# An expert layer on one core: rows gathered whole and then turned, weight pieces split in one instruction per part

## The chip, the cores and the metric

The kernel runs on one core of a Trainium2 chip. The metric is device time in microseconds: the median of the timed runs of the kernel as it stands is 1961.04 us (three runs, 1960.67 to 1962.01 us). All numbers of the profile are from one profiled execution, whose span is 1961.2 us.

## The reference

Two encoder layers over 256 tokens of width 1024. Each has a token mixer, a cross-attention into 256 memory tokens and a channel mixer, every one of them followed by a layer norm of the residual. The channel mixer of the first layer is dense; that of the second sends each token to two of eight experts. The file that is given ends with the cross-attention; the change touches the experts alone, and what they compute is this:

```
logits = x @ moe_router                # 256 tokens x 8 experts
top 2 of 8, gates = softmax of the two logits
expert e: y = (silu(x @ moe_wg[e]) * (x @ moe_wu[e])) @ moe_wd[e]
x <- LayerNorm(ALPHA * x + sum over the two experts of gate * y)
```

An expert's hidden width is 3584, so its three matrices hold 3 x 1024 x 3584 float32 numbers, 42 MiB; the eight experts hold 336 MiB, and all of it is read once.

## The kernel before

Products are made at more than the precision of TensorE's fast float32 form: a factor is held as a rounded part h and the rest l, in the type float32r, and a product is the sum of three matmuls, h by h, h by l and l by h. Weights come from memory as float32 and are split on the chip.

**Weight pieces.** `wload` (L294 to L321) loads one piece of 1 MiB (128 partitions x 2048) into the next buffer `wr` of a ring, copies it on ScalarE to the rounded part `wh` (L312) and subtracts that on VectorE to get `wl` (L316). It does so in steps of n // pieces columns; in the expert stage `pieces[0]` is `PX`, which is 4, so a piece takes four ScalarE and four VectorE instructions of 128x512. The parts have a ring of four buffers of their own, `wr` in the expert stage one of eleven: two for the whole kernel, one that held keys, five of the second layer and `NX` = 3 of this stage. SyncE issues the load when VectorE has finished with the buffer.

**Experts.** `moe` (L1270 on) ranks the experts, gives each token a slot in its expert's list, and then runs eight experts of up to 128 tokens. Per expert:

- `gather` (L1333): `pd` is a 0/1 matrix that puts tokens into slots. The tokens' two parts (`xtokh`, `xtokl`) are stationary in pieces of 128x128 and `pd` is streamed, so that the result `xg` comes out turned, features on the partitions (L1344, 32 matmuls of 128 columns); four ScalarE copies bring it to SBUF (L1346).
- `gate_up` (L1355), seven times, 512 hidden columns at a time: 48 matmuls of 512 columns on two pieces of `moe_wg` and two of `moe_wu` (L1363 to L1365), then `hs` = silu(gate) * up (ScalarE L1368, VectorE L1369).
- `down` (L1372), one step later: four transposes of `hs` (L1375), a split of the result into `hh` and `hl` (L408), 24 matmuls on two pieces of `moe_wd` into `ps_ye` (L1387 to L1389). The second piece of the very last step is put behind the split of the hidden part.
- `combine` (L1391), after the seventh: `ps_ye`, scaled by the gates, is split (`yh` ScalarE, `yl` VectorE, L1409 and L1410) and spread to the tokens (`ps_co`, L1413 and L1414), and VectorE adds it to `x` (L1417, L1419) and makes the matrix `pg` of the next combine (L1395).

A scheduler sets the order of instructions on each engine when the program is built; each engine then takes its own list strictly in order and waits on semaphores. The next expert's gather is called at step `NC - 3` of seven, and its instructions stand among those of the running expert.

Of the kernel before, what the change touches and what calls it, by code (L numbers as in the profile page):

```python
# [19 lines left out]
P = 128  # L20
# [17 lines left out]
PM, PC, PX = 2, 4, 4  # L38
# [6 lines left out]
NX = 3  # L45
# [76 lines left out]
def _tiles():  # L122
    """name -> (index, first k-tile, k-tiles, first column, columns) of the pieces in which a weight is loaded"""
    def feat(i, c0, n):
        return [(i, 0, KT, c0 + c, min(256, n - c)) for c in range(0, n, 256)]

    def tok(i, c0, n):
        return [(i, k, 4, c0 + c, min(512, n - c)) for c in range(0, n, 512) for k in (0, 4)]

    def down(i, n):  # L130
        return [(i, k, 2, 0, D) for k in range(0, n // P, 2)]

    t = {"w_in": [], "ffn_wd": down(0, D_FF)}
    for l in range(L):
        for f in (0, AW, 2 * AW):
            t["w_in"] += feat(l, f, AW)
        t["w_in"] += tok(l, 3 * AW, AW) + [(l, 0, KT, 4 * AW, 24)] + feat(l, 2968, CW)
        for c, n in ((1560, 512), (2072, 384), (2456, 512), (3224, 256)):
            t["w_in"] += tok(l, c, n)
    for n in ("xq", "xk"):  # L140
        t[n] = [x for l in range(L) for x in feat(l, 0, D)]
    for n in ("xv", "xo", "w_out"):
        t[n] = [x for l in range(L) for x in tok(l, 0, D)]
    for n in ("ffn_wg", "ffn_wu"):
        t[n] = feat(0, 0, D_FF)
    for n in ("moe_wg", "moe_wu"):
        t[n] = [x for e in range(NE) for x in tok(e, 0, FE)]
    t["moe_wd"] = [x for e in range(NE) for x in down(e, FE)]
    return t
# [13 lines left out]
def tile_encoder(ctx: ExitStack, tc: tile.TileContext, a: dict, out: bass.AP, cw: dict):  # L163
# [20 lines left out]
    def abank(name):  # L184
        """the banks of psa and psf in turn"""
        turn[0] = (turn[0] + 1) % 4
        return bank(psa, "pa", name) if turn[0] else bank(psf, "pf", name)

# [9 lines left out]
    @contextmanager  # L198
    def weights(name, bufs=2, side="left", ring=parts):
        """adds buffers to the ring of weight parts, or of weights as loaded"""  # L200
        with tc.tile_pool(name="W" + name, bufs=bufs, side=side, reuse_waits="tile") as pool:
            ring += [pool] * bufs
            yield
            ring[:] = [r for r in ring if r is not pool]
# [54 lines left out]
    def load_rest(M):  # L259
        SY.dma_start(x, a["x"].rearrange("(h p) d -> p h d", p=P))  # L260
        w = (w0 + w1) // 2
        for i, nm in enumerate(("rt32", "wm")):
            t = M.tile([P, 32, 32], F32, name=nm).rearrange("p a b -> p (a b)")[:, :w]
            SY.dma_start(t, a["consts"][:, n0 + i * w:n0 + i * w + w])
            V.tensor_copy(hm_all[:, i * w:i * w + w], t)
        rt = M.tile([P, 256], F32, name="tm32")[:, :KT * NE].rearrange("p (k e) -> p k e", k=KT)
        SY.dma_start(rt, a["moe_router"][0].rearrange("(k p) e -> p k e", p=P))
        V.tensor_copy(rth, rt)
        V.tensor_sub(rtl, rt, R_(rth))
        # lower bound of the second layer  # L270
        lbt = M.tile([P, 32, 32], F32, name="rb").rearrange("p a b -> p (a b)")[:, :2 * CW].rearrange("p (i c) -> p i c", i=2)
        SY.dma_start(lbt, a["lbl"][None].to_broadcast([P, 2, CW]))
        V.tensor_max(lb[:, 0], lbt[:, 0], lbt[:, 1])
        V.tensor_sub(lbt[:, 0], lbt[:, 0], lb[:, 0])
        V.tensor_sub(lbt[:, 1], lbt[:, 1], lb[:, 0])
        A.activation(lbt, lbt, AF.Exp)
        V.tensor_add(lb[:, 0], lbt[:, 0], lbt[:, 1])
        V.reciprocal(lb[:, 1], lb[:, 0])
        V.tensor_mul(lb[:, 0], lbt[:, 1], lb[:, 1])
        V.tensor_scalar(lb[:, 1], lb[:, 0], -1.0, 1.0, op0=OP.mult, op1=OP.add)  # L280
# [9 lines left out]
    where = _offsets()  # L290

    def wload(name, i, k0, n0, c0, n1, late=()):
        """late: instructions behind which the parts are taken"""
# [8 lines left out]
        # behind a norm only the first weights may be split before it ends  # L302
# [20 lines left out]
    def wload_halves(name, i, k0, n0, c0, n1, cols):  # L323
        """a piece of weights as two halves of its columns or of its k-tiles, in small buffers"""
        n = n0 * n1
        raw = rotate(raws).tile([P, 2048], F32, name="wr")
        at = where[name, i, k0, n0, c0, n1]
        SY.dma_start(raw[:, :n], a[name][at:at + P * n].rearrange("(p n) -> p n", p=P))
        raw = raw[:, :n].rearrange("p (a b) -> p a b", a=n0)
        for j in range(2):  # L330
            W = halves[0]
            src = raw[:, :, j * n1 // 2:(j + 1) * n1 // 2] if cols else raw[:, j * n0 // 2:(j + 1) * n0 // 2]
            m = n0 if cols else n0 // 2
            h, l = (W.tile([P, 1024], F32R, name=t)[:, :n // 2].rearrange("p (a b) -> p a b", a=m) for t in ("hh", "hl"))
            A.activation(h, src, AF.Copy)
            V.tensor_sub(l[:, :m // 2], src[:, :m // 2], R_(h[:, :m // 2]))
            G.tensor_sub(l[:, m // 2:], src[:, m // 2:], R_(h[:, m // 2:]))
            yield h, l
# [5 lines left out]
    def together(*parts):  # L344
        """interleaves generators that yield the share of their work that is done"""
# [9 lines left out]
    def later(gen, n):  # L355
        """the steps of a generator as if they stood n instructions further down"""
# [13 lines left out]
    def proj_feat_steps(name, i, c0, ncol, xh, xl, evac, bank_=None):  # L370
        """out^T[f, tok]: weights stationary"""
# [38 lines left out]
    def rms_rstd(dst, ss, n, bias=None):  # L410
        """dst = (ss / n + eps) ** -0.5"""
# [15 lines left out]
    def log_sig(dst, src):  # L427
        """dst = ln(1 + exp(-src)) = -ln(sigmoid(src))"""
# [7 lines left out]
    def mixer(l, xh, xl, kctx):  # L436
        wi = ("w_in", l)
        with tc.tile_pool(name=f"mx{l}", bufs=1, reuse_waits="tile") as M, ExitStack() as mctx:
# [32 lines left out]
            def unit(f0, n):  # L471
                """l2 norm of the heads of conv tiles f0 .. f0 + n"""
# [10 lines left out]
            def products(w, f0):  # L483
                """k of a chunk against its tiles f0 .. f0 + 3, heads of either parity in a bank"""
# [11 lines left out]
            def A1():  # L496
# [28 lines left out]
                # (I + L^T)^-1 of the 32-blocks: 96 blocks side by side on the partitions  # L525
# [34 lines left out]
            def A1c(LT, wm):  # L560
# [37 lines left out]
            def A1b(beta, ld, DB):  # L598
# [38 lines left out]
            def A2(k_t, v_t, beta, ef, cdp, fb, AT, U64, col_b):  # L637
                # u', w'^T, k decays
# [37 lines left out]
                # state recurrence  # L676
# [30 lines left out]
                # outputs  # L707
# [76 lines left out]
            # C projections  # L784
# [97 lines left out]
    def softmax_rows(M, ps, n, scale, pt):  # L882
        """ps [P, n, 256] logits in PSUM -> pt [P, n, 256] probabilities"""
# [62 lines left out]
    def mixer_c(l, MS, big, c2, g2, M, sg, qc, ci, cg, oc):  # L946
# [27 lines left out]
        # chunk decays and the decayed queries  # L974
# [17 lines left out]
        # state recurrence  # L992
# [30 lines left out]
        for hf in range(NH):  # L1023
            tok = slice(hf * P, hf * P + P)
            # at a level, the left half of a block is key to the right one going forward, and the right
            # half to the left one going backward: both directions meet in one product
# [73 lines left out]
    def affine(e, x, mean, rstd, lp):  # L1100
        """x <- (x - mean) * rstd * gain + bias"""
# [8 lines left out]
    def resid_ln(l, i, pool, srcs, rows_ready=None, parts=None):  # L1110
        """x <- LN(ALPHA x + y); srcs(add, norm) calls add(hf, c, ps) for every [P, 512] piece of y and
        norm(hf) when a half is complete. Returns x^T in two parts. rows_ready(hf): x itself is
        wanted early."""
# [33 lines left out]
    def tok_out(w, xh, xl):  # L1147
        def srcs(add, norm):
            ws = [[wload(*w, kh * 4, 4, c * 512, 512) for kh in range(2)] for c in range(2)]
            pss = [[bank(psb, "pb", "ps_t") for _ in range(2)] for _ in range(NH)]  # L1150
            # the end of the second half comes behind the first half, whose norm it covers
# [118 lines left out]
    def moe(l, i, xh, xl, xth, xtl):  # L1270
        with weights("r3", NX, ring=raws), tc.tile_pool(name="mo", bufs=1, reuse_waits="tile") as O:
# [19 lines left out]
            # experts ahead of an expert: a larger logit, or the same one and a lower index  # L1291
# [41 lines left out]
            def gather(e, sl):  # L1333
# [5 lines left out]
                for i, src in enumerate((xth, xtl)):  # L1339
                    for k0 in (0, 4):  # L1340
                        pg = bank(psb, "pb", "ps_gt").rearrange("p (k t) -> p k t", k=4)
                        for k in range(4):
                            for hf in range(NH):
                                T.matmul(pg[:, k], src[:, hf, (k0 + k) * P:(k0 + k + 1) * P], pd[:, hf],  # L1344
                                         start=hf == 0, stop=hf == NH - 1)
                        A.activation(g[:, i, k0:k0 + 4], pg, AF.Copy)  # L1346
                return g[:, 0], g[:, 1]

            def expert_run(experts, sl, late=False):
                """the down projection of a step follows the gate / up projection of the next one"""  # L1350
# [21 lines left out]
                def down(e, c, hs, ye):  # L1372
# [6 lines left out]
                    for f0 in (0, 2):  # L1379
                        # behind the last loads the hidden part goes first  # L1380
# [10 lines left out]
                def combine(e, ye, first):  # L1391
                    # a token takes the row of its slot, weighted by its gate
# [54 lines left out]
            # the statistics of the last norm are taken anew where an expert has more tokens than slots  # L1447
# [103 lines left out]
```

## Time and profile before

| | |
|---|---|
| median of the runs | 1961.04 us (1960.67 to 1962.01) |
| span of the profiled execution | 1961.2 us |
| busy: TensorE, VectorE, ScalarE, GpSimd | 94%, 80%, 65%, 13% |
| expert stage | about 926 to 1943 us of the span |
| expert stage, 1000 to 1100 us: TensorE, VectorE, ScalarE | 99.55, 92.13, 80.05 us of 100 |
| memory traffic there | 349 GB/s, DMA engines 95% busy |

The page gives busy time by engine and by group of instructions. A busy TensorE is one on which matmuls overlap, so the spacing of their starts says more than their durations. The stage of the experts is read from the windows, the waits and the timeline, since the shares of the whole span mix it with the two mixers.

### The profile page before, as it was taken

What the parts mean: (1) busy time and instruction counts of PE and PEld (TensorE: products, weight loads), DVE (VectorE), ACT (ScalarE), POOL (GpSimd) and SP (SyncE); (2) the same over time, 40 slices, a digit from 0 to 9 for tenths busy, and PEclk for the clock granted to TensorE, in tenths of its full rate; (3) what the DMA queues carried; (4) which work ended last, traced back from release to release, by engine and by line L of the source; (5) the groups of instructions that cost most, each with busy time, mean ns of one, the idle gap of its engine ahead of it and who ended that gap; (6) DMA issues with size and microseconds to landing.
All of it is one profiled execution on the core that took longest, in us unless ns stands there. A gap on an engine that the chain in (4) does not pass through costs nothing. (4 is left out here: it accounts for less than half of the span.)

```text
span 1961.2 us, 31715 instructions
## 1 busy us (share of the span) xinstructions
PE 1838.9 (94%) x11906; PEld 1544.8 (79%) x11906; DVE 1575.2 (80%) x2812; ACT 1277.4 (65%) x2559; POOL 257.4 (13%) x248
## 2 busy tenths in 40 slices
PE   6889999999979898998999999999999999999996
PEld 5778779899967777686888788887888878788784
DVE  7887665755578966665889989899899898998986
ACT  4755435555536544454788778787877877787774
POOL 4545310000036353001000000000000000000000
PEclk8988999999989888998999999999999999999998
DMA  6321255555323313552999999999999989999980
GB/s 217 111 101 67 90 190 206 176 180 185 126 81 119 103 67 108 215 215 95 350 354 354 346 357 342 354 350 350 346 350 354 351 335 358 339 353 343 347 349 23
DMA packets 71266, 473.44 MB, mean 241 GB/s; under 512 B 8768, under 2 KB 12224, under 8 KB 15936
## 3 DMA queue, kind: packets, MB, share of 16 engines
q1 hardware_dynamic: 70384, 466.09, 64.6%
q10 hardware_dynamic: 720, 5.24, 0.7%
q8 instruction: 95, 1.56, 0.3%
q14 instruction: 67, 0.55, 0.1%
HBM read 470.26 MB, written 1.05 MB: 240 GB/s over the span
## 5 line engine op out<-in xcount | busy, mean ns | idle before, releaser
L316 DVE TENSOR_TENSOR wl<-wr,wh 128x512 fp32r<-128x512 f32 (+2 forms) x1622 | 1017.6, 693 | 119.3 <-ACT wh L312 116.8
L312 ACT ACTIVATE wh<-wr 128x512 fp32r<-128x512 f32 (+1 forms) x1656 | 915.0, 630 | 241.1 <-PE ps_gu L1365 152.2
L1364 PE MATMUL ps_gu<-wl,xg 128*128 128x512 f32 x896 | 352.8, 395 | 0.1
L1363 PE MATMUL ps_gu<-wh,xg 128*128 128x512 f32 x896 | 350.9, 397 | 0.0
L1365 PE MATMUL ps_gu<-wh,xg 128*128 128x512 f32 x896 | 350.6, 392 | 0.0
L1364 PEld LDWEIGHTS ps_gu<-wl,xg 128*128 128x128 f32 x896 | 169.0, 189 | 37.8 <-DVE wl L316 2.3
L1363 PEld LDWEIGHTS ps_gu<-wh,xg 128*128 128x128 f32 x896 | 169.1, 189 | 36.8 <-ACT wh L312 0.5
L1365 PEld LDWEIGHTS ps_gu<-wh,xg 128*128 128x128 f32 x896 | 168.8, 188 | 36.9
L1387 PE MATMUL ps_ye<-wh,hh 128*128 128x512 f32 x448 | 176.7, 396 | 4.6 <-ACT hh L408 4.6
L1388 PE MATMUL ps_ye<-wl,hh 128*128 128x512 f32 x448 | 176.6, 394 | 0.0
L1389 PE MATMUL ps_ye<-wh,hl 128*128 128x512 f32 x448 | 169.8, 397 | 0.0
L319 POOL TENSOR_TENSOR wl<-wr,wh 128x384 fp32r<-128x384 f32 (+6 forms) x68 | 103.6, 1544 | 290.4 <-ACT wh L312 290.1
L1475 POOL TENSOR_TENSOR x<-x,lp 128x512 f32<-128x512 f32 x1 | 1.8, 1817 | 1029.2 <-ACT x L1474 1029.2
L1387 PEld LDWEIGHTS ps_ye<-wh,hh 128*128 128x128 f32 x448 | 84.2, 188 | 26.7 <-ACT hh L408 7.9
L1257 PE MATMUL ps_gu<-xTl,wh 128*128 128x256 f32 x352 | 99.1, 282 | 0.0
L1388 PEld LDWEIGHTS ps_ye<-wl,hh 128*128 128x128 f32 x448 | 84.3, 188 | 18.6
L1256 PE MATMUL ps_gu<-xTh,wh 128*128 128x256 f32 x352 | 98.8, 282 | 0.0
L1258 PE MATMUL ps_gu<-xTh,wl 128*128 128x256 f32 x352 | 98.8, 281 | 0.0
L1389 PEld LDWEIGHTS ps_ye<-wh,hl 128*128 128x128 f32 x448 | 82.5, 188 | 17.3
L1257 PEld LDWEIGHTS ps_gu<-xTl,wh 128*128 128x128 f32 x352 | 66.7, 189 | 0.6 <-DVE xTl L408 0.2
L1256 PEld LDWEIGHTS ps_gu<-xTh,wh 128*128 128x128 f32 x352 | 66.7, 190 | 0.5
L1258 PEld LDWEIGHTS ps_gu<-xTh,wl 128*128 128x128 f32 x352 | 66.8, 190 | 0.0
(451 smaller groups left out, 3276.9 us busy)
## 6 DMA issues: line engine op xcount, KB each, us to landing
wr<-in_moe_wg_dram SPq DMA_DIRECT2D x112, 1024.0 KB, 6.8
wr<-in_moe_wu_dram SPq DMA_DIRECT2D x112, 1024.0 KB, 6.9
wr<-in_moe_wd_dram SPq DMA_DIRECT2D x112, 1024.0 KB, 7.0
wr<-in_w_in_dram SPq DMA_DIRECT2D x16, 1024.0 KB, 4.9
wr<-in_ffn_wg_dram SPq DMA_DIRECT2D x11, 1024.0 KB, 5.2
wr<-in_ffn_wu_dram SPq DMA_DIRECT2D x11, 1024.0 KB, 5.0
wr<-in_ffn_wd_dram SPq DMA_DIRECT2D x11, 1024.0 KB, 4.9
wr<-in_xk_dram SPq DMA_DIRECT2D x8, 1024.0 KB, 4.9
```

What stands on the lines that cost most here:

```text
L312: A.activation(h[:, s], raw[:, s], AF.Copy)
L316: V.tensor_sub(l[:, m], raw[:, m], R_(h[:, m]))
L319: G.tensor_sub(l[:, m], raw[:, m], R_(h[:, m]))
L1256: T.matmul(ps[:, g], wh[:, k, fs], xh[:, k, :], start=k == 0, stop=False)
L1257: T.matmul(ps[:, g], wh[:, k, fs], xl[:, k, :], start=False, stop=False)
L1258: T.matmul(ps[:, g], wl[:, k, fs], xh[:, k, :], start=False, stop=k == KT - 1)
L1363: T.matmul(pt, gh[:, k], wh[:, k4], start=k == 0, stop=False)
L1364: T.matmul(pt, gh[:, k], wl[:, k4], start=False, stop=False)
L1365: T.matmul(pt, gl[:, k], wh[:, k4], start=False, stop=k == KT - 1)
L1387: T.matmul(ye[n], hh[:, f0 + f], dh[:, f, ns], start=b, stop=False)
L1388: T.matmul(ye[n], hh[:, f0 + f], dl[:, f, ns], start=False, stop=False)
L1389: T.matmul(ye[n], hl[:, f0 + f], dh[:, f, ns], start=False, stop=z)
```

## The change

The step count of the split in the expert stage goes from `PX` = 4 to 1: a piece takes one ScalarE and one VectorE instruction of 128x2048. `NX` goes from 3 to 2, so that the ring of loads has ten buffers. The 8 KiB per partition that this frees hold, among other things, the new tile `rows`.

`gather` now keeps `pd` stationary and streams the tokens' parts, 512 features at a time, summing the h and the l part in one bank: eight matmuls of 512 columns give an expert's tokens as whole float32 rows. Two ScalarE copies bring them to `rows`, eight transposes of 128x128 turn them, and two calls of `evac_split` (ScalarE copy and VectorE subtraction, L408) make the two parts of `xg` again. Of the rest of the diff nothing reaches the program: comments and texts are gone.

```diff
-PM, PC, PX = 2, 4, 4
+PM, PC, PX = 2, 4, 1
...
-NX = 3
+NX = 2
...
                 g = act.tile([P, 2, KT, P], F32R, name="xg", tag="opTh" if e % 2 == 0 and sl is slot else "opTl")
-                for i, src in enumerate((xth, xtl)):
-                    for k0 in (0, 4):
-                        pg = bank(psb, "pb", "ps_gt").rearrange("p (k t) -> p k t", k=4)
-                        for k in range(4):
-                            for hf in range(NH):
-                                T.matmul(pg[:, k], src[:, hf, (k0 + k) * P:(k0 + k + 1) * P], pd[:, hf],
-                                         start=hf == 0, stop=hf == NH - 1)
-                        A.activation(g[:, i, k0:k0 + 4], pg, AF.Copy)
+
+                rows = O.tile([P, D], F32, name="rows")
+                for n in range(2):
+                    ns = slice(n * 512, n * 512 + 512)
+                    pg = bank(psb, "pb", "ps_gr")
+                    for i, src in enumerate((xth, xtl)):
+                        for hf in range(NH):
+                            T.matmul(pg, pd[:, hf], src[:, hf, ns], start=i + hf == 0, stop=i + hf == NH)
+                    A.activation(rows[:, ns], pg, AF.Copy)
+                for k0 in (0, 4):
+                    pg = bank(psb, "pb", "ps_gt").rearrange("p (k t) -> p k t", k=4)
+                    for k in range(4):
+                        T.transpose(pg[:, k], rows[:, (k0 + k) * P:(k0 + k + 1) * P], ident)
+                    evac_split(g[:, 0, k0:k0 + 4], g[:, 1, k0:k0 + 4], pg)
                 return g[:, 0], g[:, 1]
```

Up to the first gather every engine has the same list as before. From there the scheduler's order differs. Six lines are added in `gather`, so that what stood on L1363 stands on L1369 now, and so on to the end. Three places follow, each first as it was and then as it is.

VectorE where the expert stage begins, from the first expert's `pd` on (`m` and `cnt` are small tiles of the router, `pg` belongs to the first combine). Before:

```order
874 L1336 TENSOR_SCALAR pd<-consts,slot 128x128
875 L316 TENSOR_TENSOR wl<-wr,wh 128x512 x4
876 L1325 TENSOR_REDUCE cnt<-cnt 128x1
877 L316 TENSOR_TENSOR wl<-wr,wh 128x512 x8
878 L1336 TENSOR_SCALAR pd<-consts,slot 128x128
879 L316 TENSOR_TENSOR wl<-wr,wh 128x512 x2
880 L1308 TENSOR_SCALAR m_9780<-m_9780 128x2
```

Now:

```order
874 L1336 TENSOR_SCALAR pd<-consts,slot 128x128
875 L316 TENSOR_TENSOR wl<-wr,wh 128x2048 x3
876 L1336 TENSOR_SCALAR pd<-consts,slot 128x128
877 L1325 TENSOR_REDUCE cnt<-cnt 128x1
878 L1336 TENSOR_SCALAR pd<-consts,slot 128x128
879 L316 TENSOR_TENSOR wl<-wr,wh 128x2048
880 L1308 TENSOR_SCALAR m_9780<-m_9780 128x2
881 L1401 TENSOR_SCALAR pg<-consts,slot 128x128 x2
882 L408 TENSOR_TENSOR xg<-ps_gt,xg 128x512 x2
```

VectorE had no part in the first gather but `pd`; now it makes the l part of `xg` (row 882), and four splits of whole pieces stand ahead of that.

VectorE where one expert ends and the next is under way (the first of seven such places). Before:

```order
922 L316 TENSOR_TENSOR wl<-wr,wh 128x512 x12
923 L1410 SCALAR_TENSOR_TENSOR yl<-ps_ye,gs,yh 128x512 x2
924 L316 TENSOR_TENSOR wl<-wr,wh 128x512 x4
925 L1417 SCALAR_TENSOR_TENSOR x<-x,ps_co 128x512 x2
926 L316 TENSOR_TENSOR wl<-wr,wh 128x512
927 L1417 SCALAR_TENSOR_TENSOR x<-x,ps_co 128x512
928 L316 TENSOR_TENSOR wl<-wr,wh 128x512
929 L1417 SCALAR_TENSOR_TENSOR x<-x,ps_co 128x512
930 L1395 TENSOR_SCALAR pg<-consts,slot 128x128 x2
931 L316 TENSOR_TENSOR wl<-wr,wh 128x512 x6
```

Now:

```order
921 L316 TENSOR_TENSOR wl<-wr,wh 128x2048 x3
922 L1416 SCALAR_TENSOR_TENSOR yl<-ps_ye,gs,yh 128x512 x2
923 L316 TENSOR_TENSOR wl<-wr,wh 128x2048
924 L1423 SCALAR_TENSOR_TENSOR x<-x,ps_co 128x512 x4
925 L1401 TENSOR_SCALAR pg<-consts,slot 128x128 x2
926 L316 TENSOR_TENSOR wl<-wr,wh 128x2048 x2
```

The quarter pieces that stood between the additions to `x` are gone; the four additions and `pg` stand in one block ahead of the next whole piece.

TensorE at the end of the last expert (`ps_pT` is the turned `pg` of the last combine). Before:

```order
8160 L1389 MATMUL ps_ye<-wh,hl 128x512
8161 L1387 MATMUL ps_ye<-wh,hh 128x512
8162 L1388 MATMUL ps_ye<-wl,hh 128x512
8163 L1389 MATMUL ps_ye<-wh,hl 128x512
8164 L1387 MATMUL ps_ye<-wh,hh 128x512
8165 L1375 MATMUL ps_hT<-consts,hs 128x128 x4
8166 L1398 MATMUL ps_pT<-gate,pg 128x1 x2
8167 L1388 MATMUL ps_ye<-wl,hh 128x512
```

Now:

```order
8196 L1371 MATMUL ps_gu<-wh,xg 128x512
8197 L1381 MATMUL ps_hT<-consts,hs 128x128 x4
8198 L1404 MATMUL ps_pT<-gate,pg 128x1 x2
8199 L1406 MATMUL ps_pT<-consts,pg 128x128 x2
8200 L1393 MATMUL ps_ye<-wh,hh 128x512
8201 L1394 MATMUL ps_ye<-wl,hh 128x512
8202 L1393 MATMUL ps_ye<-wh,hh 128x512
```

The last step's transposes stood behind 20 matmuls of the step before; now they follow the last gate and up matmul at once.

## Rows read from the trace of the kernel before

**Rows 1.** Windows: stretch and length in us, then busy us by engine.

```profile
core 0: us, PE busy (x) PEld busy (x) DVE busy (x) ACT busy (x) POOL busy (x), PEclk, DMA share, GB/s
920.00:940.00 20.00, 16.25 (x74) 14.51 (x72) 15.84 (x51) 11.30 (x23) 2.76 (x2) 0.65 0.60 222
1000.00:1100.00 100.00, 99.55 (x462) 81.58 (x461) 92.13 (x155) 80.05 (x153) 0.00 (x0) 1.00 0.95 349
1915.00:1940.00 25.00, 24.89 (x116) 20.00 (x114) 17.86 (x30) 14.24 (x29) 0.00 (x0) 1.00 0.00 1
```

**Rows 2.** Waits, 930 to 1930 us: total us, times, longest us.

```profile
ACT wh L312 <- PE ps_gu L1365: 152.2, 133, 4.5
DVE wl L316 <- ACT wh L312: 74.3, 80, 3.2
PEld ps_ye L1387 <- ACT hh L408: 7.9, 8, 1.6
```

**Rows 3.** Timeline of TensorE, sixth and seventh expert: start, us, work, count.

```profile
1775.00 0.40 PE L1363 MATMUL ps_gu<-wh,xg 128*128 128x512 f32 x1
...
1781.16 0.39 PE L1363 MATMUL ps_gu<-wh,xg 128*128 128x512 f32 x1
1781.39 1.90 PE L1344 MATMUL ps_gt<-pd,xtokl 128*128 128x128 f32 x16
1783.12 0.45 PE L1364 MATMUL ps_gu<-wl,xg 128*128 128x512 f32 x1
```

**Rows 4.** Timeline of TensorE, three transposes inside the last expert.

```profile
1916.31 0.49 PE L1375 MATMUL ps_hT<-consts,hs 128*128 128x128 f32 x3
...
1916.87 0.39 PE L1365 MATMUL ps_gu<-wh,xg 128*128 128x512 f32 x1
```

**Rows 5.** Groups by shape: count | busy us, mean ns | idle us before, releasers.

```profile
L316 DVE TENSOR_TENSOR wl<-wr,wh 128x512 fp32r<-128x512 f32 x1588 | 984.3, 687 | 108.3 <-ACT wh L312 106.0 <-DMA wr<-in_moe_wd_dram 1.2
L408 DVE TENSOR_TENSOR x0l<-xt,x0h 128x1024 fp32r<-128x1024 f32 x2 | 2.5, 1226 | 6.3 <-ACT x0h L408 6.3
L312 ACT ACTIVATE wh<-wr 128x512 fp32r<-128x512 f32 x1608 | 871.8, 621 | 230.1 <-PE ps_gu L1365 152.2 <-PE ps_ye L1389 24.1 <-PE ps_gu L1257 18.6
L312 ACT ACTIVATE wh<-wr 128x1024 fp32r<-128x1024 f32 x36 | 36.0, 1051 | 9.1 <-PE ps_gu L1257 4.2 <-PE ps_f L385 3.3 <-DMA wr<-in_w_in_dram 1.5
```

**Rows 6.** Timeline of VectorE where the first expert ends.

```profile
1076.05 1.41 DVE L1410 SCALAR_TENSOR_TENSOR yl<-ps_ye,gs,yh 128x512 fp32r<-128x512 f32 x2
1077.37 2.49 DVE L316 TENSOR_TENSOR wl<-wr,wh 128x512 fp32r<-128x512 f32 x4
1079.78 1.28 DVE L1417 SCALAR_TENSOR_TENSOR x<-x,ps_co 128x512 f32<-128x512 f32 x2
1080.97 0.68 DVE L316 TENSOR_TENSOR wl<-wr,wh 128x512 fp32r<-128x512 f32 x1
...
1083.38 0.48 DVE L1395 TENSOR_SCALAR pg<-consts,slot 128x128 f32<-128x128 f32 x2
1083.77 3.69 DVE L316 TENSOR_TENSOR wl<-wr,wh 128x512 fp32r<-128x512 f32 x6
```

**Rows 7.** Timelines of TensorE and VectorE where the expert stage begins.

```profile
926.21 0.66 PE L1344 MATMUL ps_gt<-pd,xtokh 128*128 128x128 f32 x2 [0.82 <-DVE slot L1329]
...
933.07 0.73 PE L1363 MATMUL ps_gu<-wh,xg 128*128 128x512 f32 x1
933.60 0.63 PE L1364 MATMUL ps_gu<-wl,xg 128*128 128x512 f32 x1
934.03 0.63 PE L1363 MATMUL ps_gu<-wh,xg 128*128 128x512 f32 x1
...
937.44 0.47 PE L1363 MATMUL ps_gu<-wh,xg 128*128 128x512 f32 x1
...
926.40 2.49 DVE L316 TENSOR_TENSOR wl<-wr,wh 128x512 fp32r<-128x512 f32 x4
...
936.43 0.28 DVE L1336 TENSOR_SCALAR pd<-consts,slot 128x128 fp32r<-128x128 f32 x1
```

**Rows 8.** Timeline of ScalarE, the last piece of weights.

```profile
1932.73 0.60 ACT L408 ACTIVATE hh<-ps_hT 128x512 fp32r<-128x512 f32 x1 [2.98 <-PE ps_hT L1375]
1933.22 2.18 ACT L312 ACTIVATE wh<-wr 128x512 fp32r<-128x512 f32 x4
```

## What the change was predicted to do

> **What bounds the kernel now.** I read the windows first: in the expert stage TensorE is busy 99.55 us of 100 at a granted clock of 1.00 (2.4 GHz), VectorE 92.13, ScalarE 80.05, with the DMA engines 95% busy [rows 1]. Then the waits, to see who is late: ScalarE waits 152.2 us for TensorE to free a buffer of weight parts and VectorE 74.3 us for ScalarE, while TensorE's weight loads wait 7.9 us in all, eight times, for `hh` [rows 2]. So weights are split as fast as TensorE lets go of buffers, and TensorE sets the time. Then TensorE's timeline, for the price of its work by the spacing of starts, since matmuls overlap: 27 matmuls of 512 columns between 1775.00 and 1781.16 us, 0.228 us each; 16 gather matmuls of 128 columns from 1781.39 to 1783.12, 0.108 each [rows 3]; three transposes and one matmul of 512 in 0.56 us, so 0.11 for a transpose [rows 4].
>
> A piece of weights is used by 12 matmuls, 2.74 us. With four buffers of parts, a buffer that is freed has to be full again three pieces later, 8.2 us. What the change does to the time turns on this slack, not on VectorE's total.
>
> **1. The gather on TensorE.** Before, 32 x 0.108 = 3.46 us an expert [rows 3]. After, 8 matmuls of 512 and 8 transposes: 8 x 0.228 + 8 x 0.11 = 2.70 [rows 3, 4]. Seven of the eight gathers lie inside a busy TensorE: 7 x 0.76 = **5.3 us less**. ScalarE has two copies and two `xg` copies instead of four copies, the same. VectorE gets two subtractions of 0.6 us an expert, hidden as long as it has slack; priced below where it has none.
>
> The spacing of 0.108 us at 128 columns is almost half that at 512. The Trainium skill, page "TensorE: Matmul & The Clock Gate", section "Back-to-back issue gap", gives N / 2.4 + 2.5 ns for a lone gap, 56 ns at 128 columns and 216 ns at 512. By that the old gather would take 1.79 us and the new one 2.17, and the change would cost 2.7 us there instead of saving 5.3. The row at 512 agrees within 6%, that at 128 is twice the page's figure, so the measurement decides.
>
> **2. The split in one instruction.** No 128x2048 split is in the trace. VectorE takes 687 ns at 512 columns and 1226 at 1024 [rows 5], 539 ns per 512 more, hence 2.30 us alone at 2048. In a queue the next starts a little earlier: four of 512 take 2.41 us from start to start [rows 6]. I take 2.22; bounds 2.13 (1226 ns and 1024 columns more at 0.45) and 2.41 (no gain at all). ScalarE takes 621 and 1051 ns [rows 5], so 1051 + 2 x 430 = 1.91; I take 1.9, bounds 1.7 and the 2.18 of four in a row [rows 8]. Over 336 pieces VectorE loses about 336 x 0.2 = 67 us of busy time, but it is not what TensorE waits for, so I book nothing.
>
> What counts is latency. TensorE could start on a piece when its first quarter was split, about 0.53 + 0.60 us after ScalarE began; now it has to have the whole, 1.9 + 2.22.
>
> **3. The seven places where one expert follows another.** There VectorE has most to do besides splits [rows 6]. From the order: 12 `ps_ye` matmuls before an expert's end a buffer is freed. From then VectorE's chain is: ScalarE's split 1.9, split 2.22, two `yl` 1.32, split 2.22, four additions to `x` 4 x 0.595 = 2.38, two `pg` 0.39, split 2.22 = 12.65 us. TensorE has in that stretch 45 matmuls of 512 and 4 transposes: 45 x 0.228 + 4 x 0.11 = 10.70. So it waits about 2.0 us. Five of the seven stand like this. At the ends of the fourth and the fifth expert one more whole split stands ahead of `yl`: 2.0 + 2.2 = 4.2. Sum 5 x 2.0 + 2 x 4.2 = 18.4. At two other places of the stage, with 3.45 us of matmuls against 4.1 of the two splits, some 2.5 us in all. Against that TensorE's waits of before, 7.9 us [rows 2], stand in the same places and are covered by the longer ones. Net **13 us more**. With 2.13 and 1.7 for the splits the chain is 0.5 shorter, with 2.41 and 2.18 it is 0.85 longer; times seven, 9.5 to 19.
>
> **4. The start.** Before, VectorE's work for the first gather ended with `pd`, and TensorE began the experts at 933.07 us; after ten matmuls at 0.427 us (the 0.65 of the window, the level of 1.2 GHz) it ran at 2.4 GHz from 937.44 [rows 1, 7]. Now the l part of the first `xg` comes from VectorE behind four whole splits. From 926.40 [rows 7]: three splits 6.66, `pd` and `cnt` 0.45, split 2.22, `m` and `pg` 0.46, one subtraction 0.6 = 936.8 us. TensorE does its gather, the transposes and four matmuls by about 933.3 and then waits some 3.5 us. Of the ten matmuls that it had done by 937.44, it has four, so it has 6 x 0.427 = 2.6 us to make up; the new gather's first part is shorter, and the slow clock may last longer. I take **2.8 us more**, from 1 (the wait is filled by work that can go ahead) to 5 (ten more matmuls at 0.427 instead of 0.228).
>
> **5. The end.** TensorE ran there without a gap, 24.89 us of 25 [rows 1]. Now the last gate and up matmuls want a piece whose buffer is freed 12 matmuls earlier: 2.74 us against 1.9 + 2.22 + 0.6 (VectorE's `hs` product in between) = 4.72, a wait of 1.98. The last `moe_wd` piece stands behind `hh`: 0.58 + 1.9 + 2.22 = 4.70 against 4 `ps_pT` 0.44 and 14 x 0.228 = 3.63, a wait of 1.07; before, it came as four quarters in 2.18 [rows 8]. Together **3.1 us more** (2 to 4.5).
>
> **6. The ring of ten.** A load waits for VectorE to be done with a buffer; one buffer fewer is one piece less ahead, 3 us of some 30. Loads are held up by VectorE's pace and not the other way (one wait of VectorE for a load in the stage, 1.2 us [rows 5]). Nothing booked; its price if the cover is gone is one piece, 3 us.
>
> **Sum.** -5.3 + 13 + 2.8 + 3.1 = +13.6 on a span of 1961.2 us, which differs from the median of 1961.04 by 0.2: about **1975 us**. Own range: terms 3 to 5 at their low ends and nothing else give 1968, at their high ends 1984.
>
> **Rivals.** (A, faster.) The waits of term 3 vanish, those of before as well: the 67 us that VectorE is spared give it room to run ahead, so that at an expert's end the parts of all four buffers stand ready. For it: VectorE is busy 92% [rows 1]. Against it: four buffers are all there is, and running ahead ends when they are full; it decides when ScalarE's and VectorE's split together come below some 2.1 us, half of what rows 5 give, or when the chain of 12.65 holds one split fewer than I count, 10.4 against 10.70. Then -5.3 - 7.9 + 2.8 + 3.1 = -7.3: 1954. Chance 0.12.
> (B, faster, VectorE sets the pace.) If TensorE's matmuls are paced by the splits that feed them, the 67 us come out of the time: 1961 - 67 = 1894. The 152.2 us that ScalarE waits for TensorE [rows 2] speak against it. The Trainium skill, page "VectorE: DVE Perf Modes", section "The TRN2 errata — SBUF-src ops pay a fixed extra latency per instruction", says that one large tile pays that latency once and many small ones pay it each; the rows agree with a fixed part (1226 is less than twice 687), and by that rule the change is a gain wherever VectorE is the bound. Chance 0.03.
> (C, no change.) The waits at the boundaries are only those of before, moved from `hh` to the parts: -5.3 + 2.8 + 3.1 = +0.6: 1962. It decides when the chain is 1 us shorter than I count, which an order of VectorE kept by the chip with shorter gaps would do. Chance 0.14.
> (D, slower.) The loads become late with ten buffers and each expert pays one piece, 8 x 3 = 24 us on top: 1999. The DMA engines are 95% busy [rows 1], but the queue moves when VectorE frees a buffer, and TensorE's pace is unchanged. Chance 0.04.
> (E, the page's rule on lone gaps holds for the old gather.) It would be 2.7 - (-5.3) = 8 us more than my sum: 1983. The 16 spacings of 0.108 us [rows 3] speak against it. Chance 0.02.
>
> **How the numbers follow.** My forecast has 0.65. About 0.2%, 3.9 us, is what a measurement of this kernel can tell from no change, so faster means below 1957 and slower above 1965. A and B are faster, 0.15; C is the same, 0.14, and the low end of my own range adds 0.01; the rest is slower, 0.70. The range of 8 in 10 takes in my own range, C and the upper half of A: 1955 to 1986. What is left out is B, D and half of A, and the error of terms I did not see.
>
> **What would show it.** In the trace of the changed kernel: at each of seven places TensorE waits some 2 us (two of them 4) for `wl` from VectorE (term 3; no such wait would make A or C right); a spacing of 0.228 elsewhere and a gather of 2.7 us (term 1); VectorE's split of 2.2 to 2.3 us and its busy share down to about 86 of 100 (term 2); a wait of 3.5 us at about 933 us with the clock low for longer (term 4); two waits in the last 20 us, for `hs` and for the last piece's parts (term 5); loads that land well before ScalarE takes them (term 6). VectorE waiting for DMA would make D right.

## The result and the profile after

| | before | changed |
|---|---|---|
| median of the runs | 1961.53 us (4 runs, 1960.67 to 1962.76) | 1975.73 us (4 runs, 1974.99 to 1979.19) |
| ratio, 95% interval | | 1.008 (1.0066 to 1.0094) |
| span of the profiled execution | 1961.2 us | 1973.7 us |
| first gather matmul starts at | 926.21 us | 920.99 us |
| first gather matmul to last `ps_ye` matmul | 1013.3 us | 1031.3 us |

The change costs 0.8%, and the forecast was 1975. The two spans understate what happened among the experts: in the changed kernel's profiled execution everything ahead of the first gather took 5.2 us less. All of that was there at the first instruction that differs, ScalarE's first copy of an expert's piece, which stands a little ahead of the first gather and starts at 913.60 us instead of 918.82. So that part varies by itself: in thirteen of the fourteen profiled executions of this study the instructions ahead of that copy are the same (run 12 is the exception), and the first gather matmul starts between 920.6 and 928.6 us. For this reason the stage is compared from its own start: 18.0 us more, where the prediction's sum was 13.6.

Windows of the changed kernel, columns as in [rows 1]: the start, the middle, the end of the stage.

```profile
920.00:945.00 25.00, 20.10 (x72) 15.27 (x73) 17.34 (x30) 11.51 (x12) 0.00 (x0) 0.83 0.57 211
1000.00:1100.00 100.00, 97.51 (x438) 78.82 (x437) 84.91 (x56) 70.04 (x51) 0.00 (x0) 1.00 0.92 343
1930.00:1955.00 25.00, 22.55 (x94) 17.22 (x92) 13.01 (x11) 9.53 (x10) 0.00 (x0) 0.93 0.00 1
```

VectorE went from 92.13 to 84.91 us of 100 and ScalarE from 80.05 to 70.04 [rows 1]: both have less to do. TensorE, which sets the time, went from 99.55 to 97.51. Waits of the changed kernel from 930 to 1945 us:

```profile
ACT wh L312 <- PE ps_gu L1371: 216.5, 181, 9.1
DVE wl L316 <- ACT wh L312: 154.2, 198, 6.0
...
PEld ps_gu L1370 <- DVE wl L316: 21.9, 21, 2.0
...
PEld ps_gu L1371 <- DVE xg L408: 3.5, 1, 3.5
...
PE ps_hT L1381 <- DVE hs L1375: 2.2, 1, 2.2
```

Beside [rows 2]: ScalarE and VectorE wait longer than before (216.5 and 154.2 us for 152.2 and 74.3), so neither is short of time on the whole, and yet TensorE's weight loads now wait 21 times for VectorE's `wl`. The latency grew while the load fell. The prices, by groups (compare [rows 5]):

```profile
L316 DVE TENSOR_TENSOR wl<-wr,wh 128x2048 fp32r<-128x2048 f32 x336 | 765.6, 2289 | 155.7 <-ACT wh L312 155.4
L312 ACT ACTIVATE wh<-wr 128x2048 fp32r<-128x2048 f32 x336 | 643.3, 1920 | 289.6 <-PE ps_gu L1371 216.5 <-PE ps_ye L1395 68.1 <-ACT hh L408 1.9
```

**A boundary.** The end of the first expert: ScalarE's copy into the freed buffer, VectorE's timeline, then the two matmuls of TensorE's that waited:

```profile
1070.04 1.92 ACT L312 ACTIVATE wh<-wr 128x2048 fp32r<-128x2048 f32 x1 [0.84 <-PE ps_ye L1395]
...
1071.99 2.29 DVE L316 TENSOR_TENSOR wl<-wr,wh 128x2048 fp32r<-128x2048 f32 x1 [0.46 <-ACT wh L312]
1074.20 1.40 DVE L1416 SCALAR_TENSOR_TENSOR yl<-ps_ye,gs,yh 128x512 fp32r<-128x512 f32 x2
1075.52 2.28 DVE L316 TENSOR_TENSOR wl<-wr,wh 128x2048 fp32r<-128x2048 f32 x1
1077.72 2.47 DVE L1423 SCALAR_TENSOR_TENSOR x<-x,ps_co 128x512 f32<-128x512 f32 x4
1080.11 0.47 DVE L1401 TENSOR_SCALAR pg<-consts,slot 128x128 f32<-128x128 f32 x2
1080.51 2.28 DVE L316 TENSOR_TENSOR wl<-wr,wh 128x2048 fp32r<-128x2048 f32 x1
...
1074.34 0.50 PE L1370 MATMUL ps_gu<-wl,xg 128*128 128x512 f32 x1 [0.70 <-DVE wl L316]
...
1082.84 0.50 PE L1370 MATMUL ps_gu<-wl,xg 128*128 128x512 f32 x1 [0.85 <-DVE wl L316]
```

The chain of term 3 is there link by link. ScalarE takes the freed buffer at 1070.04 us and VectorE is done at 1082.79: 12.75 us, forecast 12.65. The wait came in two parts: TensorE stands still once for the first split of the chain and once for the last. By the spacing of starts, with what is lost around each wait, that is 2.28 us here; forecast 2.0. At the ends of the fourth and the fifth expert the standstill is split over two engines: at the fourth TensorE stands 1.36 us for ScalarE's `yh`, which is behind two whole copies, then 0.40 us for a `wh`, then 1.75 us for VectorE's `wl`. VectorE's chain is the forecast one all the same: it runs without a gap, and from ScalarE's copy at 1451.19 us to its end at 1466.15 it takes 14.96 us, where 12.65 and one more split of 2.22 are 14.87.

**The start**, TensorE and VectorE (compare [rows 7]):

```profile
927.91 0.50 PE L1370 MATMUL ps_gu<-wl,xg 128*128 128x512 f32 x1 [0.77 <-DVE wl L316]
931.64 0.55 PE L1371 MATMUL ps_gu<-wh,xg 128*128 128x512 f32 x1 [3.22 <-DVE xg L408]
...
934.97 0.58 PE L1370 MATMUL ps_gu<-wl,xg 128*128 128x512 f32 x1
935.39 0.39 PE L1371 MATMUL ps_gu<-wh,xg 128*128 128x512 f32 x1
...
928.24 2.28 DVE L316 TENSOR_TENSOR wl<-wr,wh 128x2048 fp32r<-128x2048 f32 x1
...
930.90 1.28 DVE L408 TENSOR_TENSOR xg<-ps_gt,xg 128x512 fp32r<-128x512 f32 x2
```

Four matmuls, then a standstill until VectorE has made the l part of `xg` behind its splits, then eight spacings of 0.427 us, the clock's lower level, and 0.23 from 935.39 on.

**The end:**

```profile
1941.40 0.39 PE L1371 MATMUL ps_gu<-wh,xg 128*128 128x512 f32 x1
1943.98 0.66 PE L1381 MATMUL ps_hT<-consts,hs 128*128 128x128 f32 x4 [2.19 <-DVE hs L1375]
...
1946.04 0.63 PE L1393 MATMUL ps_ye<-wh,hh 128*128 128x512 f32 x1
1946.46 0.63 PE L1394 MATMUL ps_ye<-wl,hh 128*128 128x512 f32 x1
```

One wait of 2.6 us between starts, and then, which was not forecast, seven spacings of 0.427 us: after this standstill TensorE runs at the lower level again (0.93 in the window above).

### The profile page after: what moved, and what is told of

Read it like the earlier page. It is cut to its first block, busy times and chain, and to the rows that moved or that the text cites. A ratio compares the mean times of both kernels' runs of the same rounds, so it can differ in the third digit from the quotient of the medians.

```text
span 1973.7 us, 29403 instructions
## 1 busy us (share of the span) xinstructions
PE 1830.6 (93%) x11778; PEld 1527.5 (77%) x11778; DVE 1525.1 (77%) x1820; ACT 1196.5 (61%) x1551; POOL 256.8 (13%) x248
## 5 line engine op out<-in xcount | busy, mean ns | idle before, releaser
L316 DVE TENSOR_TENSOR wl<-wr,wh 128x2048 fp32r<-128x2048 f32 (+3 forms) x614 | 957.0, 1587 | 198.3 <-ACT wh L312 197.5
L312 ACT ACTIVATE wh<-wr 128x2048 fp32r<-128x2048 f32 (+2 forms) x648 | 832.9, 1319 | 352.1 <-PE ps_gu L1371 216.5
L1369 PE MATMUL ps_gu<-wh,xg 128*128 128x512 f32 x896 | 351.2, 397 | 0.9 <-ACT wh L312 0.8
L1369 PEld LDWEIGHTS ps_gu<-wh,xg 128*128 128x128 f32 x896 | 168.4, 188 | 39.3 <-ACT wh L312 2.0
```

The source lines that it names most:

```text
L312: A.activation(h[:, s], raw[:, s], AF.Copy)
L316: V.tensor_sub(l[:, m], raw[:, m], R_(h[:, m]))
L1369: T.matmul(pt, gh[:, k], wh[:, k4], start=k == 0, stop=False)
```

## The experiments

Each ratio is to runs of the kernel before on the same chip, with its 95% interval; medians of the kernel before were 1960.41 us for runs 1 to 4, 1958.84 for 5 to 8, 1960.62 for 9 to 11 and 1960.10 for 12. "Stage" is the stretch of the profiled execution from the 48th gate and up matmul of the first expert to the last `ps_ye` matmul: 993.5 us before, 1009.1 changed; "start" is the stretch from the first gather matmul to that 48th one: 19.8 before, 22.2 changed.

| run | edit | median us | ratio | start | stage |
|---|---|---|---|---|---|
| 1 | before, PX 1 | 1976.74 | 1.0071 (1.0054 to 1.0088) | 19.6 | 1009.2 |
| 2 | new gather, ten buffers, PX 4 | 1965.87 | 1.0022 (1.0010 to 1.0033) | 22.9 | 994.3 |
| 3 | before, ten buffers | 1969.23 | 1.0038 (1.0026 to 1.0050) | 19.6 | 1002.4 |
| 4 | changed, additions of 64 columns | 1974.06 | 1.0060 (1.0038 to 1.0081) | 22.2 | 1006.5 |
| 5 | before, nine buffers | 1965.55 | 1.0031 (1.0019 to 1.0044) | 19.6 | 998.7 |
| 6 | before, PX 2 | 1965.15 | 1.0031 (1.0022 to 1.0040) | 19.9 | 997.9 |
| 7 | run 2, first gather old | 1957.38 | 0.9987 (0.9979 to 0.9996) | 19.8 | 992.3 |
| 8 | run 7, PX 2, gather earlier, two `hs` | 1950.91 | 0.9961 (0.9947 to 0.9975) | 19.9 | 985.8 |
| 9 | run 1, five parts buffers, nine loads | 1965.47 | 1.0025 (1.0016 to 1.0035) | 19.6 | 1000.1 |
| 10 | run 8, PX 1 | 1971.04 | 1.0052 (1.0037 to 1.0066) | 19.6 | 1004.8 |
| 11 | changed, VectorE in quarters | 1988.28 | 1.0145 (1.0128 to 1.0163) | 22.9 | 1019.3 |
| 12 | before, another priority | 1959.30 | 0.9993 (0.9984 to 1.0002) | 19.8 | 991.0 |

**Run 1: whole pieces alone.**

```diff
-PM, PC, PX = 2, 4, 4
+PM, PC, PX = 2, 4, 1
```

> The kernel before with PX = 1 alone (old gather, eleven load buffers). My theory, that the whole-piece split costs TensorE its waits at the seven expert boundaries and in the last 20 us: no 5.3 us of gather gain, little lost at the start because the old gather takes nothing from VectorE, so 13 + 3.1 + about 0.5 = 16 to 17 us slower than before, with waits for wl at the boundaries. Rival, that the two new VectorE subtractions of each gather are what makes VectorE late: without them at most +8 us. Also open: the part ahead of the experts took 5.2 us less in the changed kernel's profile (first gather matmul at 920.99 us, not 926.21); if that comes with the order or the number of split instructions in the stage it shows here too, if from the ring of ten or from the gather it does not.

16 us, as the theory had it, without any of the new gather's work on VectorE. The split alone costs what the whole change costs, within the intervals. The waits of TensorE's weight loads for `wl`, in the kernel before from 940 to 1935 us:

```profile
PEld ps_gu L1364 <- DVE wl L316: 2.3, 6, 0.5
```

and in this run from 945 to 1935 us:

```profile
PEld ps_gu L1364 <- DVE wl L316: 19.6, 22, 1.6
```

Six of the seven boundaries have two waits each, like the first one of the changed kernel; the first has one. Some 4 of the 16 us are of another kind, which the theory did not have: once, at 1029.62 us inside the first expert, TensorE's next start comes 2.76 us later because it waits for `hh`, and slower spacings follow. Run 3 shows that pattern.

**Run 2: the gather without whole pieces.** The changed kernel with `PX = 4`.

> The new gather with ten load buffers, split in quarters as before (PX = 4; with eleven buffers the tile rows does not fit). My theory: 5.3 us less on TensorE, the boundaries as before, and up to 3 us lost at the start because the first xg's low part waits behind VectorE's quarters: 2 to 5 us faster than before, seven gathers at 2.7 us each in the trace, boundary waits as in the kernel before. Rival one, that the gather's extra VectorE work is what costs: waits at the boundaries like those of the changed kernel, and slower than before by some 5 us. Rival two, the rule of N / 2.4 + 2.5 ns for lone gaps: gather 0.4 us longer each.

5.5 us slower, not faster. The gather itself did what was forecast: by the spacings of starts the seven later gathers take 18.2 us of TensorE instead of 23.8. TensorE's weight loads wait 6.1 us for `wl` here and 21.9 in the changed kernel, so the gather's own work on VectorE is not what makes the boundaries late. The start took 3.1 us more, as term 4 had it. What is left over, some 8 us (5.5 - 3.1 + 5.6), is neither, and that is what the next run is about.

**Run 3: ten load buffers alone.**

```diff
-NX = 3
+NX = 2
```

> The kernel before with ten load buffers instead of eleven and nothing else. My theory: loads are far enough ahead, within 1 us of before. Rival: each expert loses up to a piece of 3 us, up to 24 us slower, with VectorE or ScalarE waiting for loads. If the 5.2 us that the changed kernel gained ahead of the expert stage come from the smaller ring, this kernel shows them and is about 5 us faster.

8.8 us slower, and the rival's number, but not the rival's cause: no wait of ScalarE or VectorE for a load stands in the stage at all, and the first three boundaries lose 1.0 us each, as before. TensorE's list is that of before up to 1450 us; from the fourth boundary on the order differs, and what the stage loses it loses behind that. At the sixth, ScalarE and TensorE:

```profile
1714.01 2.19 ACT L312 ACTIVATE wh<-wr 128x512 fp32r<-128x512 f32 x4 [0.98 <-PE ps_gu L1365]
1716.10 0.58 ACT L1368 ACTIVATE hs<-ps_gu 128x512 f32<-128x512 f32 x1
1716.58 0.58 ACT L408 ACTIVATE hh<-ps_hT 128x512 fp32r<-128x512 f32 x1
...
1714.04 0.60 PE L1375 MATMUL ps_hT<-consts,hs 128*128 128x128 f32 x4
1717.22 0.51 PE L1387 MATMUL ps_ye<-wh,hh 128*128 128x512 f32 x1 [2.58 <-ACT hh L408]
1717.56 0.40 PE L1388 MATMUL ps_ye<-wl,hh 128*128 128x512 f32 x1
```

ScalarE's `hh`, for which TensorE has its transposes ready, stands behind four quarters that wait for TensorE to free their buffer. TensorE stands 2.58 us for it, and seven spacings of 0.427 us follow.

**Run 4: shorter additions.**

```diff
-                            xs = x[:, hf, ns]
+                            xs = x[:, hf, n * 512:n * 512 + 64]
+                            po = po[:, :64]
```

> The changed kernel with the additions to x in the combine cut from 512 to 64 columns each (448 of 512 columns of every addition are left out). My theory, that the boundary waits are VectorE's chain from the freed buffer on (12.65 us against 10.70 of matmuls, in which four additions are 2.38): the chain falls by about 1.8 to 2 us, so the waits of some 2 us at the boundaries shrink to near nothing, 10 to 14 us faster than the changed kernel, 1961 to 1966. Rival, that the wait is the latency of ScalarE's and VectorE's whole split alone, whatever else VectorE has to do: unchanged within 3 us, about 1973 to 1976.

Only 1.7 us faster than the changed kernel: the number is a miss. The trace says in part why. VectorE and TensorE where the first expert ends:

```profile
1083.09 0.35 DVE L1424 SCALAR_TENSOR_TENSOR x<-x,ps_co 128x64 f32<-128x64 f32 x2
...
1084.68 2.29 DVE L316 TENSOR_TENSOR wl<-wr,wh 128x2048 fp32r<-128x2048 f32 x1
...
1086.85 0.48 PE L1369 MATMUL ps_gu<-wh,xg 128*128 128x512 f32 x1
1087.16 0.40 PE L1370 MATMUL ps_gu<-wl,xg 128*128 128x512 f32 x1
```

The second wait of this boundary (0.85 us at 1082.84 in the changed kernel) is gone, as the chain demands; the first, for the split at its head, has nothing to do with the additions and stays (0.70). But the edit also changed the scheduler's order from the first expert on, and other waits came up inside the experts: TensorE's weight loads still wait 18.6 us for `wl`, and VectorE waits 12.2 us for four loads, where in the changed kernel it waits for none. The chain is confirmed at this place; over the stage the run can't price it.

**Run 5: nine load buffers.**

```diff
-NX = 3
+NX = 1
```

> The kernel before with nine load buffers instead of eleven. With ten it was some 8 us slower, though no load was waited for, and TensorE's rows were those of before until the fourth expert's end. Theory order: a smaller ring only changes the order that the scheduler makes, so nine buffers give another order and another time, not a steadily longer one: 0 to 10 us slower than before, no wait of ScalarE or VectorE for a load above 3 us in all. Rival loads: each buffer less makes loads later, so nine cost at least twice what ten cost, 16 to 24 us slower, with waits for loads in the trace.

6.7 us slower, less than ten buffers cost, with no wait for a load. So loads that come late are not the cause. That the different order is the cause has been read from run 3's trace; no run shows it by changing the order there alone.

**Run 6: half pieces.** `PX = 2`.

> The kernel before with PX = 2 alone (two instructions of 128x1024 a part). Theory latency: TensorE needs a half of a piece instead of a quarter or the whole; the delay ahead of the first part is 1.05 + 1.15 = 2.2 us, between 1.13 (quarters) and 4.1 (whole), a third of the way, so about a third of the 16 us that PX = 1 alone cost, 3 to 7 us slower. Rival chain: VectorE's chain at the boundaries decides, and as it is 10.7 us long there is room for one more half, so 0 to 3 us slower. Rival order: the whole instruction as such is harmless and the order that goes with PX = 1 cost the 16 us; then anything between -5 and +10.

6.3 us, inside the range of the latency theory, but the rival of order allowed it too, and the trace bears the theory out only in part. Six of the seven boundaries have one spacing of 1.6 us ahead of a `wl`, and lose together some 2 us more than in the kernel before. The seventh shows run 3's pattern, a spacing of 2.66 us ahead of a matmul with `hh` and slower spacings behind it, and loses some 3 us more than before. So more than half of what halves cost in the stage (4.5 us) is not the latency that the theory priced.

**Run 7: the first gather as it was.**

```diff
+                if e == 0:
+                    for i, src in enumerate((xth, xtl)):
...
+                else:
+                    rows = O.tile([P, D], F32, name="rows")
...
```

> The new gather with ten buffers and quarters, as in the second run, but the first expert's gather is the old one. Theory start: what the new gather loses at the start (the first 48 gate matmuls end 22.9 us after the gather's first matmul, not 19.8) comes back, 3 us less than the 1965.9 of that run: 1962 to 1964, and in the trace no 3 us wait for xg at the start. Rival: the order of the rest changes as well and hides it, 1960 to 1970.

The start is back at 19.8 us and the 3 us wait for `xg` is gone. The median fell by 8.5 us, by the ratios 0.35% or 7 us, more than the 3 forecast, and lies below both ranges: 2 us of the rest lie in the stage, what is left was not found.

**Run 8: the parts that helped.** Against run 7:

```diff
-PM, PC, PX = 2, 4, 4
+PM, PC, PX = 2, 4, 2
...
-HSB = 1
+HSB = 2
...
-                        if c == NC - 3 and n + 1 < len(experts):
+                        if c == NC - 4 and n + 1 < len(experts):
```

> A version made from the parts that helped: old gather for the first expert, the new one for the other seven and called a step earlier (four steps ahead of the next expert), pieces split in two halves (PX = 2), ten load buffers and a second buffer for hs in the room that this leaves. Theory: 5.3 us less by the gathers, nothing lost at the start, boundary waits of 7 to 10 us as before or fewer: 1950 to 1958. Rival, that the half pieces and ten buffers cost as much as they did alone: 1962 to 1972.

1950.91 us, 0.39% below the kernel before and inside the forecast. Three things were changed at once against run 7, so the run does not tell which of them helped. TensorE has no gap in the window that [rows 1] shows for the kernel before:

```profile
1000.00:1100.00 100.00, 100.00 (x454) 81.91 (x453) 89.99 (x92) 74.79 (x86) 0.00 (x0) 1.00 0.96 357
```

**Run 9: a fifth buffer of parts for whole pieces.** Against the kernel before:

```diff
-PM, PC, PX = 2, 4, 4
+PM, PC, PX = 2, 4, 1
...
-NX = 3
+NX = 1
...
-        with weights("r3", NX, ring=raws), tc.tile_pool(name="mo", bufs=1, reuse_waits="tile") as O:
+        with weights("r3", NX, ring=raws), weights("c3", 1), tc.tile_pool(name="mo", bufs=1, reuse_waits="tile") as O:
```

> Whole pieces (PX = 1) and the old gather as in the first run, but five buffers of weight parts instead of four, paid for with two load buffers (nine left). Theory latency: TensorE waits at the boundaries because a freed buffer has to be whole again within three pieces, 8.2 us; with a fifth buffer it has 11 us, and the waits for wl from VectorE (19.9 us of weight loads, 23 times, in the first run) fall below 4 us; the time falls by 8 to 14 us from that run's 1977, to 1963 to 1969, less what the order with nine load buffers costs (up to 7 us). Rival, that VectorE as such is too slow there: the waits for wl stay above 12 us and the time at 1974 or more.

This run bears most on the cause: 11.3 us less than run 1 (9 by the ratios), with VectorE's instructions as they were, and the same time as nine load buffers with quarters (run 5, 1965.55). With one more buffer the cost of whole pieces is gone or nearly so. Two limits: the order changed here too, and quarters with five buffers were not run, so what a fifth buffer is worth to quarters is open. The waits for `wl` in the stretch of run 1's line:

```profile
PEld ps_gu L1364 <- DVE wl L316: 4.4, 5, 1.4
```

**Run 10: whole pieces in the mixed version.** `PX = 1`.

> The mixed version of the eighth run with whole pieces (PX = 1) instead of halves, nothing else changed. Theory latency: the same cost as whole pieces had between the kernel before and the first run or between the second run and the changed kernel, 10 to 16 us, of it 3 in the last 20 us: 1961 to 1967 where halves took 1951. Rival order: the cost came with that order alone, and here whole pieces are within 4 us of halves.

20 us more (18 by the ratios), so the cost does not belong to one order; it is above the forecast, and three boundaries (the second, fourth and sixth) show run 3's pattern as well, 2.3 us between starts ahead of a matmul with `hh`.

**Run 11: ScalarE whole, VectorE in quarters.**

```diff
+            if name.startswith("moe_w"):
+                A.activation(h, raw, AF.Copy)
+                c = 512
             for s in (slice(j, j + c) for j in range(0, n, c)):
-                A.activation(h[:, s], raw[:, s], AF.Copy)
+                if not name.startswith("moe_w"):
+                    A.activation(h[:, s], raw[:, s], AF.Copy)
```

> The changed kernel with VectorE's part of the split in four instructions again and ScalarE's in one. Theory latency: ScalarE's whole instruction delays the first part by 1.9 - 0.5 = 1.4 us, VectorE's by 2.2 - 0.6 = 1.6; with VectorE in quarters about half of what whole pieces cost goes: 1966 to 1972. Rival, that ScalarE's whole instruction alone is the cost (VectorE cannot begin before it ends): 1974 to 1980, with VectorE's waits for ScalarE as long as in the changed kernel (154 us). Rival, that VectorE's alone is: 1960 to 1966.

None of the three: 12.6 us slower than the changed kernel. TensorE and ScalarE at the first boundary:

```profile
1080.04 0.60 PE L1385 MATMUL ps_hT<-consts,hs 128*128 128x128 f32 x4
1083.22 0.79 PE L1397 MATMUL ps_ye<-wh,hh 128*128 128x512 f32 x1 [2.58 <-ACT hh L412]
1083.82 0.63 PE L1398 MATMUL ps_ye<-wl,hh 128*128 128x512 f32 x1
...
1086.63 0.40 PE L1375 MATMUL ps_gu<-wh,xg 128*128 128x512 f32 x1
...
1080.29 1.91 ACT L312 ACTIVATE wh<-wr 128x2048 fp32r<-128x2048 f32 x1 [2.46 <-PE ps_gu L1375]
1082.11 0.58 ACT L1378 ACTIVATE hs<-ps_gu 128x512 f32<-128x512 f32 x1
1082.58 0.59 ACT L412 ACTIVATE hh<-ps_hT 128x512 fp32r<-128x512 f32 x1
```

It is run 3's pattern with a whole piece: `hh` stands behind a split of 1.91 us that itself waits 2.46 us for a buffer. It comes at all seven boundaries. The run can't divide the latency between the two engines, since the order changed with it.

**Run 12: only the order.**

```diff
-WQ = 0
+WQ = 100
```

> The kernel before with one number changed, the priority at which the scheduler places the splits of weights in the expert stage (0 to 100 instructions ahead): the same instructions and the same buffers, in another order. Theory order: the order at the boundaries alone moves the time by several us, so this is off by 2 to 6 us, here likely faster since splits placed earlier leave less to do at a boundary, 1955 to 1959. Rival, that the order as such does nothing and only buffers and the size of pieces count: within 1 us of before.

Not told from no change (interval 0.9984 to 1.0002). The stage is 2.5 us shorter in the trace, with other waits at other places, and the expected 2 to 6 us are not shown. The edit also reaches further than the expectation says: `WQ` holds for every split outside the token mixers, and the engines' lists differ from before long ahead of the experts, TensorE's from about 245 us on.

## Why the prediction was right, and where it was not

The time was right, 1975 for 1975.73, and so was the step that carries it: the wait at the boundaries, link by link. Not all of the terms were.

1. **Gather on TensorE, -5.3 us:** measured -5.9 (17.97 us for seven gathers, 23.85 before, by the spacings of starts). Right. The rival of lone gaps, which would have made the new gather the longer one, is out.
2. **Prices:** VectorE 2.29 us alone and 2.2 from start to start, ScalarE 1.92. Right, and right that the busy time saved is worth nothing: VectorE fell by 7 us in 100 while the kernel grew, which also rules out rival B.
3. **Boundaries, 18.4 us at seven places:** by the spacings 2.28, 2.29, 2.33, 4.5, 4.5, 2.30 and 1.96, together some 20. Right, down to the two places of 4; a fifth buffer took most of the waits for `wl` away (run 9). That rules out rivals A and C, which needed no such waits. The other places inside the experts were put at two with 2.5 us, which does not follow from the prediction's own figures (4.1 less 3.45 is 0.65 at each, 1.3 in all), and there are eight, with some 5 us. So net +13 was too small: all that TensorE lost to spacings more than 0.06 us over 0.23 and 0.11, from the 48th gate and up matmul to 30 us ahead of the last one, went from 13.7 to 32.1 us, +18.4. This is the term that was mis-sized most.
4. **Start, +2.8:** measured +2.4; in run 2 +3.1, in run 7 nothing.
5. **End, +3.1 in two waits:** one wait of 2.4 us and some 1.5 us of lower clock behind it; where the wait for the last piece was forecast, TensorE works at the slower spacing and does not stand still. By the measure of term 3 the last 30 us lose 5.1 us, 0.6 before: +4.5, the upper bound of the forecast (2 to 4.5), part of it by another road.
6. **Ring of ten, nothing:** this step was wrong for the ring alone. The prediction put the ring's price at one piece if loads came late, and rightly held that they would not: in the changed kernel ScalarE waits 1.4 us for loads, at two places, and VectorE for none, which rules out rival D. It did not ask whether a smaller ring changes the order that the scheduler makes. Alone the ring cost 0.38%. That would account for run 2 (5.6 us less by the gathers, 3.1 more at the start, 8.8 more by the ring are 6.3 more, measured 5.5), but it is not a fixed price: run 7 has the same ring and the new gather and is 0.13% faster than before. What the ring costs in the changed kernel is open. Run 1 has 0.71% and run 2 0.22%, together 0.93%, and the change 0.80%: the same within the intervals.

The sum of the stage was 13.6 and its measured cost 18.0 us in the profiled execution. The median's difference is 14.2, by the ratio 15.7. That it is smaller may come from the stretch ahead of the stage, whose time varies; four runs of each kernel do not show it. A forecast that meets the median within 1 us is here partly luck.

Open: how much of run 3's 8.8 us is order alone. Run 5 shows that it is not loads, run 3's trace shows where it is lost, but the one run that changed an order and nothing else (12) moved the time by less than can be told, and it did not change the order at that place alone.

## What to carry to other kernels

Fewer and larger instructions free the engine that makes a buffer and lengthen the time until its first part can be used; ask which of the two the engine in front waits for. Where it waits for latency, count from the instant that a buffer is freed, link by link on the engine that fills it, and set the sum against what the consumer still has in hand: here 12.65 against 10.70 us gave the loss at a boundary before the run, and one more buffer took most of it away. Where a scheduler sets the order, a change of a buffer count is a change of order too, and has to be looked at as one.

## What the runs showed of the hardware

A short standstill of TensorE can cost more than its length. After waits of 2.58 us (runs 3 and 11) six or seven spacings of 0.427 us follow, the lower of the clock's two levels, some 1.3 us on top; after the wait of 0.85 us in the changed kernel one spacing of 0.34 follows and then 0.23 again. The length of the standstill alone does not decide it: in run 10 TensorE waits 1.82 us for `hh` at 1211.83 and again at 1723.12 us, both times behind the same kind of work; eight spacings of 0.427 us follow soon after the first (granted clock 0.65 from 1212.5 to 1215 us) and none after the second (1.00 from 1723.5 to 1726). So a loss of this kind can be there or not in one and the same trace. And the time of the same instructions ahead of the experts differed by 8 us between profiled executions, so that a stage is best compared from its own start.
